# Turning attention probabilities outside TensorE: block transposes on VectorE and shifted copies on ScalarE

## The chip, the core and the metric

The kernel runs on one core of a Trainium2 chip. A core has TensorE (PE, the matrix engine; its weight loads are a row of their own, PEld), VectorE (DVE), ScalarE (ACT), GpSimd (POOL) and SyncE (SP, which here only issues DMAs). Each engine takes its instructions strictly in the order in which they were written for it, and waits where a semaphore tells it to. The metric is device time in microseconds. Three runs of the kernel before gave a median of 993.96 us (993.37 to 994.55).

## The reference

A decoder trunk of two layers on 256 tokens of width 2048, in float32: one Mamba-2 layer, then one sliding-window attention layer. Each is followed by a residual, DeepNorm scaling and a LayerNorm. The change lies wholly in the attention layer (and in the residual's affine part that runs beside it):

```python
def _swa_sink_attention(q, k, v, sinks):      # 256 tokens = 2 blocks of WINDOW = 128
    ...
    kk = jnp.concatenate([jnp.pad(kb, pad)[:, :-1], kb], axis=2)   # keys: block before, own block
    s = jnp.einsum("bcqhrd,bckhd->bchrqk", qb, kk).astype(jnp.float32) * (hd ** -0.5)
    ...
    valid = (diff >= 0)[None] & (diff < WINDOW)[None] & (kpos >= 0)
    s = jnp.where(valid[None, :, None, None], s, -jnp.inf)
    m = jnp.maximum(jnp.max(s, axis=-1, keepdims=True), sk)
    p = jnp.exp(s - m)
    p = p / (jnp.sum(p, axis=-1, keepdims=True) + jnp.exp(sk - m))
    o = jnp.einsum("bchrqk,bckhd->bcqhrd", p.astype(vv.dtype), vv)
...
    o = o * jax.nn.silu(gate)                 # in _swa_mixer
    return o @ w_out
```

There are 32 query heads of 64 in 4 groups (j = 0 to 3) of 8; each group shares one K/V head. In the first block a query sees only keys up to itself in that block. In the second block it sees 128 keys, some in the block before and the rest in its own. For every query exactly 128 key columns are live, and the second block packs the two parts into one 128-wide row.

## The kernel before, in words

**Products.** All large products are made in three passes of a split float32: a weight unit of 128 x 2048 is loaded (SP), ScalarE rounds it into a high part (`wh`, line 161), VectorE subtracts to get the low part (`wl`, line 164), and TensorE multiplies high by high, low by high and high by low (lines 249, 320 to 322, 973). There are four buffers each for `wh` and `wl`, and the weights are asked for two units ahead of the one in use. ScalarE and VectorE so have a standing duty for every unit, and TensorE takes the units one after the other.

**The attention layer** walks through `B_ORDER`: for each group j a `q` block (four units: the query projection), a `g` block (four units: the gate), and an `o` block (four units: the output projection), in the order q0 g0 q1 g1 o0 q2 g2 o1 q3 g3 o2 o3. After each unit, `tick()` counts down a list of delayed steps (`later(n, step)`), and so the attention steps of a group are put between two units of large products some ticks later. A tile scheduler then writes each engine's instructions in one fixed order.

**The attention steps of group j** (`attend(j, h)`, h = 0 and 1 for the two token blocks):

- Scores: 8 matmuls (h = 0, line 1090) or 16 (h = 1, line 1097) into PSUM tiles of the kind `ax`, of which there are four. This text calls them QK0 and QK1.
- h = 0: VectorE adds the mask on the way out of PSUM (line 1104). h = 1: ScalarE copies (line 1111), VectorE overwrites by predicate (line 1114).
- Softmax: VectorE takes the row maximum (1121) and three tiny steps (1122 to 1124), ScalarE makes eight exponentials with row sums (1127), VectorE adds, inverts and multiplies (1130 to 1132). This is `p`: queries on partitions, 8 heads x 128 keys along the row.
- Turn (`turn_p`, line 1136): the product with V needs keys on partitions. TensorE transposes eight 128 x 128 tiles against an identity (line 1140) into PSUM; VectorE and ScalarE take them out (1149, 1151 for h = 0; for h = 1 VectorE masks them twice, once for each of the two key blocks, line 1144) into tiles `pt`. This text calls the two turns of a group turn 0 and turn 1.
- PV (`pv`, line 1154): product with V (1161 for h = 0; 1178 and 1185 for h = 1), then VectorE multiplies by half the gate into `o` (1164, 1191), and ScalarE and VectorE split `o` into `oH` and `oL` for the output projection (1200, 1201).

**The residual** of the first LayerNorm's affine part (`residual`, lines 1022 and 1023) takes eight VectorE pairs between the units; its rows are fetched by POOL's DMA queue into a single pair of buffers `gb`.

## Time and profile before

| what | value |
|---|---|
| median of three runs | 993.96 us |
| the profiled execution | 993.77 us |
| its span, first to last instruction | 991.8 us |
| granted TensorE clock | 1.000 |
| busy: PE, PEld, DVE, ACT, POOL | 985.8, 897.4, 775.2, 566.5, 105.4 us |
| turns of probabilities on TensorE (line 1140) | 64 transposes in 8 turns, 8.4 us |

Times in a trace are counted from the start of the span. Rows of instruction groups name line, engine, operation, output and input tiles with buffer numbers left out, and shapes. A row of the timeline gives the start, the length and, in brackets, the idle time in front and what ended it. Matmuls overlap each other: a recorded length is longer than the distance to the next one, so TensorE's price of a step is read from distances between starts, or from the chain of waits, which counts each stretch of time once.

### The profile page before, as it was taken

What the parts mean: (1) busy time and instruction counts of PE and PEld (TensorE: products, weight loads), DVE (VectorE), ACT (ScalarE), POOL (GpSimd) and SP (SyncE); (2) the same over time, 40 slices, a digit from 0 to 9 for tenths busy, and PEclk for the clock granted to TensorE, in tenths of its full rate; (3) what the DMA queues carried; (4) which work ended last, traced back from release to release, by engine and by line L of the source; (5) the groups of instructions that cost most, each with busy time, mean ns of one, the idle gap of its engine ahead of it and who ended that gap; (6) DMA issues with size and microseconds to landing.
All of it is one profiled execution on the core that took longest, in us unless ns stands there. A gap on an engine that the chain in (4) does not pass through costs nothing.

```text
span 991.8 us, 18106 instructions
## 1 busy us (share of the span) xinstructions
PE 985.8 (99%) x7132; PEld 897.4 (90%) x7132; DVE 775.2 (78%) x1206; ACT 566.5 (57%) x992; POOL 105.4 (11%) x130
## 2 busy tenths in 40 slices
PE   9999999999999999999999999999999999999997
PEld 8999989999999998999999999888998978978976
DVE  7888897877786887686787687889688786686696
ACT  7585866547646654664664664566455544544542
POOL 0000303004003002100300300303100000000003
PEclk9999999999999999999999999999999999999999
DMA  9688577575576666656657466456754646456432
GB/s 363 241 270 328 164 262 223 172 236 176 193 232 187 219 207 196 208 180 209 208 170 236 139 203 215 157 178 223 253 185 154 192 159 197 158 159 196 158 128 86
DMA packets 61557, 198.90 MB, mean 201 GB/s; under 512 B 6848, under 2 KB 11360, under 8 KB 61216
## 3 DMA queue, kind: packets, MB, share of 16 engines
q1 hardware_dynamic: 58528, 188.53, 57.8%
q0 software_dynamic: 2336, 8.69, 2.7%
q8 instruction: 56, 0.92, 0.4%
q10 hardware_dynamic: 608, 0.52, 0.2%
q14 instruction: 29, 0.24, 0.1%
HBM read 195.49 MB, written 2.23 MB: 199 GB/s over the span
## 4 chain that ended last, share of the span: by engine, by line
PE 99%; DVE 0%; DVEq 0%; issue 0%
PE mm L249 53%; PE mm L973 11%; PE mm L320 9%; PE mm L321 9%; PE mm L322 9%; PE ax L628 2%; PE ax L604 1%; PE ax L1097 1%; PE ax L1090 0%; PE ax L587 0%; PE mm L387 0%; PE ax L1161 0%; PE ax L1140 0%; PE ax L1051 0%; PE ax L1178 0%; PE mm L1140 0%
## 5 line engine op out<-in xcount | busy, mean ns | idle before, releaser
L164 DVE TENSOR_TENSOR wl<-wr,wh 128x1024 fp32r<-128x1024 f32 (+2 forms) x338 | 393.1, 1182 | 103.6 <-ACT wh L161 101.5
L161 ACT ACTIVATE wh<-wr 128x1024 fp32r<-128x1024 f32 (+2 forms) x338 | 332.1, 1010 | 193.4 <-issue 69.1
L249 PE MATMUL mm<-xH,wh 128*128 128x256 f32 x1280 | 355.4, 278 | 0.0
L249 PE MATMUL mm<-xL,wh 128*128 128x256 f32 x1280 | 354.0, 277 | 0.0
L249 PE MATMUL mm<-xH,wl 128*128 128x256 f32 x1280 | 353.9, 277 | 0.0
L249 PEld LDWEIGHTS mm<-xH,wh 128*128 128x128 f32 x1280 | 240.4, 188 | 1.9 <-issue 0.5
L249 PEld LDWEIGHTS mm<-xL,wh 128*128 128x128 f32 x1280 | 240.6, 188 | 1.0
L249 PEld LDWEIGHTS mm<-xH,wl 128*128 128x128 f32 x1280 | 240.5, 188 | 0.2 <-DVE wl L164 0.2
L320 PE MATMUL mm<-wh,yH 128*128 128x512 f32 x256 | 101.4, 396 | 0.0
L321 PE MATMUL mm<-wh,yL 128*128 128x512 f32 x256 | 99.8, 390 | 0.0
L322 PE MATMUL mm<-wl,yH 128*128 128x512 f32 x256 | 99.7, 389 | 0.0
L644 POOL TENSOR_TENSOR yz<-yz,z 128x256 f32<-128x256 f32 x32 | 32.8, 1033 | 468.9 <-DVE yz L639 468.9
L249 PE MATMUL mm<-x1H,wh 128*128 128x256 f32 x256 | 71.7, 280 | 0.0
L491 DVE SCALAR_TENSOR_TENSOR cv<-mm,pc,cv 128x255 f32<-128x255 f32 x144 | 68.6, 477 | 3.3 <-ACT cv L489 1.9
L249 PE MATMUL mm<-x1L,wh 128*128 128x256 f32 x256 | 70.8, 277 | 0.0
L249 PE MATMUL mm<-x1H,wl 128*128 128x256 f32 x256 | 70.8, 276 | 0.0
L973 PE MATMUL mm<-wh,x1H 128*128 128x512 f32 x160 | 62.9, 393 | 0.0
L973 PE MATMUL mm<-wl,x1H 128*128 128x512 f32 x160 | 61.8, 389 | 0.0
L973 PE MATMUL mm<-wh,x1L 128*128 128x512 f32 x160 | 60.9, 389 | 0.0
L320 PEld LDWEIGHTS mm<-wh,yH 128*128 128x128 f32 x256 | 48.1, 188 | 10.3 <-DVE z L580 0.9
L322 PEld LDWEIGHTS mm<-wl,yH 128*128 128x128 f32 x256 | 48.0, 188 | 10.2
L321 PEld LDWEIGHTS mm<-wh,yL 128*128 128x128 f32 x256 | 48.1, 188 | 9.0
(226 smaller groups left out, 1346.8 us busy)
## 6 DMA issues: line engine op xcount, KB each, us to landing
wr<-in_wa SPq DMA_DIRECT2D x154, 512.0 KB, 5.0
wr<-in_wo SPq DMA_DIRECT2D x64, 512.0 KB, 4.4
wr<-in_wq SPq DMA_DIRECT2D x32, 512.0 KB, 4.5
wr<-in_wg SPq DMA_DIRECT2D x31, 512.0 KB, 4.7
wr<-in_wb SPq DMA_DIRECT2D x16, 512.0 KB, 4.1
wr<-in_wb SPq DMA_DIRECT2D x32, 256.0 KB, 3.7
rb<-rscr SPq DMA_DIRECT2D x11, 512.0 KB, 4.1
wr<-in_wkv SPq DMA_DIRECT2D x8, 512.0 KB, 4.9
```

The source lines that it names most:

```text
L161: m = nc.scalar.activation(h[:, sl], v, AF.Copy)
L164: m = nc.vector.tensor_tensor(l[:, sl], v, h[:, sl].bitcast(F32), ALU.subtract)
L249: m = nc.tensor.matmul(ps, a, b, start=first and i == 0, stop=last and i == 2)
L320: pinned(nc.tensor.matmul(ps, aH[:, k, hs], u.h[:, ks], start=k == 0 and add is None, stop=False), pin)
L321: pinned(nc.tensor.matmul(ps, aL[:, k, hs], u.h[:, ks], start=False, stop=False), pin)
L322: pinned(nc.tensor.matmul(ps, aH[:, k, hs], u.l[:, ks], start=False, stop=k == 3), pin)
L491: nc.vector.scalar_tensor_tensor(a[:, sft:], ps[:, : S - sft], w(3 - sft), a[:, sft:], ALU.mult, ALU.add)
L604: nc.tensor.transpose(ps[:, o : o + P], st.xs[i][:, c * P : (c + 1) * P], ident)
L628: nc.tensor.matmul(ps[64 * r : 64 * r + 64, cols], xd[:, c, r, :], e[:, 256:] if c else e[:, :256], start=c == 0, stop=c == 1,)
L644: nc.gpsimd.tensor_tensor(v, v, st.z[i][:], ALU.mult)
L973: m = nc.tensor.matmul(ps[:], (x1H, x1L, x1H)[i][:, kk, hs], (u.h, u.h, u.l)[i][:, ks], start=(kk, i) == (0, 0), stop=ui == 3 and (k, i) = ...
L1097: nc.tensor.matmul(pss[par][qs, at : at + 192], q2[rows, b + i, qs], kT[rows, j, 64 * part : 64 * part + 192], start=True, stop=True,)
```

## The change

In seven of the eight turns (all but j = 3, h = 1) TensorE makes no transposes. Instead:

- `p` is written in another arrangement: block column c (32 keys) outermost, then head, then key within the block. Softmax works on a strided view of it.
- VectorE turns every 32 x 32 block in place with one instruction per turn, from `p` to `z`, 128 x 1024 (`turn_far`, the STREAM_TRANSPOSE rows below). After that each block holds keys on partitions, but a block (query rows i, key columns c) still sits on the partitions of i.
- ScalarE copies each block to the partitions of c: one copy of 32 x 256 per pair (i, c); 16 for h = 1, and 10 for h = 0, where blocks above the diagonal are zero and are cleared once by three GpSimd memsets in a tile that is kept for this (`first_pt`).
- For h = 1 VectorE then makes the two masked parts from one SBUF tile (two instructions of 128 x 1024) where it made four of 128 x 512 from PSUM. For h = 0 the two copies out of PSUM (VectorE 1151, ScalarE 1149) are gone.
- The factor 0.5 of the gate moves into the reciprocal (one tiny VectorE instruction more per turn), and `o` is a plain product.
- Both PV products of a group now stand at the same tick (`PV_AT`), later than before for h = 0.
- The residual's steps are at other ticks (`RES_AT`), and its rows are fetched some ticks ahead of use (`GB_AT`, `load_affine`).
- Buffers: `p` and `z` share three, `o` takes the place of the query tiles `qt`, the bias rows have one buffer in place of two, and the last LayerNorm's temporary tiles use the tiles of the turn.

The last turn keeps TensorE's transposes, and writes its masked parts in the new arrangement. The diff, cut to its core:

```diff
-NPT = 6
 B_ORDER = [("q", 0), ("g", 0), ("q", 1), ("g", 1), ("o", 0), ("q", 2), ("g", 2), ("o", 1),
            ("q", 3), ("g", 3), ("o", 2), ("o", 3)]
 
-RES_AT = [1, 2, 3, 4, 9, 10, 11, 12]
+RES_AT = [2, 3, 6, 7, 11, 12, 14, 15]
+MOVE_AT, MASK_AT = [2, 2, 3, 3], 4
+PV_AT = [[8, 5], [5, 4]]
+GB_AT = [0, 4, 8, 13]
 ALPHA = (2.0 * 2) ** 0.25
...
+    def load_affine(c):
+        for i, n in enumerate(("lng", "lnb")):
+            gb1[i] = bp.tile([P, 512], F32, tag=f"gb{i}", name=nm("gb1"), bufs=1)
+            nc.gpsimd.dma_start(gb1[i][:], A[n][0, c * 512 : (c + 1) * 512].partition_broadcast(P))
     def residual(c, h):
 
-        if h == 0:
-            for i, n in enumerate(("lng", "lnb")):
-                gb1[i] = bp.tile([P, 512], F32, tag=f"gb{i}", name=nm("gb1"), bufs=1)
...
     gb1 = {}
+    load_affine(0)
     for c in range(4):
+        if c:
+            later(GB_AT[c], lambda c=c: load_affine(c))
         for h in range(2):
...
+    def first_pt():
+        if not firsts:
+            t = bp.tile([P, 4, 8, 32], F32, tag="pt0", name="pt0", bufs=1)
+            for c in range(1, 4):
+                nc.gpsimd.memset(t[32 * c : 32 * c + 32, :c].rearrange("p c r a -> p (c r a)"), 0.0)
+            firsts.append(t)
+        return firsts[0]
...
-        p = bp.tile([P, 8, P], F32, tag=f"p{h}", name=nm("p"), bufs=1)
+        p = bp.tile([P, 1024], F32, tag="p", name=nm("p"), bufs=3)
+        far = j < 3 or h == 0
+        byhead = p[:].rearrange("p (c r b) -> p r c b" if far else "p (r c b) -> p r c b", r=8, c=4)
...
-                v = p[:, par * 4 + b : par * 4 + b + per, :]
+                v = byhead[:, par * 4 + b : par * 4 + b + per]
+                got = pss[par][:].rearrange("p (a k) -> p a k", a=per)
                 if h == 0:
                     nc.vector.tensor_tensor(
...
+                        v, blocks(got), blocks(mask_a0.unsqueeze(1)).to_broadcast([P, per, 4, 32]), ALU.add
                     )
...
-        nc.vector.tensor_reduce(mx, p[:], AX.X, ALU.max)
+        nc.vector.tensor_reduce(mx, byhead, AX.XY, ALU.max)
...
             nc.scalar.activation(
-                p[:, r, :], p[:, r, :], AF.Exp, bias=ng[:, r : r + 1], accum_out=rs[:, r : r + 1]
+                byhead[:, r], byhead[:, r], AF.Exp, bias=ng[:, r : r + 1], accum_out=rs[:, r : r + 1]
             )
...
         nc.vector.reciprocal(ri, rs)
-        nc.vector.tensor_tensor(p[:], p[:], ri.unsqueeze(2).to_broadcast([P, 8, P]), ALU.mult)
+        nc.vector.tensor_scalar(ri, ri, 0.5, None, ALU.mult)
+        nc.vector.tensor_tensor(
+            byhead, byhead, ri.unsqueeze(2).unsqueeze(3).to_broadcast([P, 8, 4, 32]), ALU.mult
...
+        def turn_far():
+            z = bp.tile([P, 4, 256], F32, tag="p", name=nm("z"), bufs=3)
+            nc.vector.transpose(z[:].rearrange("p c f -> p (c f)"), p[:])
+            if h == 0:
+                pts[0] = first_pt()
+            else:
+                for kc in range(2):
+                    pts[kc] = bp.tile([P, 4, 8, 32], F32, tag=("pri", "own")[kc], name=nm("pt"), bufs=1)
+            def moved(c):
+                for i in range(c * (h == 0), 4):
+                    nc.scalar.copy(
+                        pts[0][32 * c : 32 * c + 32, i].rearrange("p r a -> p (r a)"), z[32 * i : 32 * i + 32, c]
+                    )
+            def parts():
+                t, own = (pts[kc][:].rearrange("p c r b -> p r c b") for kc in range(2))
+                for kc, d in ((1, own), (0, t)):
+                    nc.vector.tensor_tensor(d, t, masked(kc, 8), ALU.mult)
+            for c in range(4):
+                later(MOVE_AT[c], lambda c=c: moved(c))
+            if h:
+                later(MASK_AT, parts)
         def turn_p():
+            for kc in range(2):
+                pts[kc] = bp.tile([P, 4, 8, 32], F32, tag=("pri", "own")[kc], name=nm("pt"), bufs=1)
             for par in range(2):
-                pt = ax_tile() if h else mm_tile()
+                pt = ax_tile()
                 for a in range(4):
-                    nc.tensor.transpose(pt[:, a * P : (a + 1) * P], p[:, par * 4 + a, :], ident)
...
-                            (anti, tri)[kc].unsqueeze(1).to_broadcast([P, 4, P]), ALU.mult,
...
+                got = blocks(pt[:].rearrange("p (a q) -> p a q", a=4))
+                for kc in range(2):
+                    t = pts[kc][:].rearrange("p c r b -> p r c b")[:, par * 4 : par * 4 + 4]
+                    nc.vector.tensor_tensor(t, got, masked(kc, 4), ALU.mult)
...
+            def gated(ov, q0, n):
+                at = slice(h * P + q0, h * P + q0 + n)
+                nc.vector.tensor_tensor(
+                    blocks(o[:, :, q0 : q0 + n]), ov.rearrange("p (c a b) -> p a c b", a=4, b=32),
+                    blocks(sg[j][:, :, at]), ALU.mult,
+                )
...
                 for par in range(2):
...
                     )
...
+                gated(ov[:], 0, P)
...
-        last = j == 3
-        later(4 if last and h == 0 else 3, turn_p)
-        later((5 if last else 6) if h == 0 else (8 if 0 < j < 3 else 4), pv)
+        if far:
+            turn_far()
+        else:
+            later(3, turn_p)
+        later(PV_AT[j == 3][h], pv)
         if h == 0:
-            later(1 if last else 3, lambda: attend(j, 1))
+            later(1 if j == 3 else 3, lambda: attend(j, 1))
```

What the scheduler makes of it is seen at three places.

TensorE, group 0. Before, turn 1 stands right behind the first PV (line 1161), and the second PV stands a unit later, with the query transposes of group 1 (line 1051) behind it (`ax`: PSUM tiles, `pt`: turned probabilities, `cc`: the identity, `mm` ... `x1H`: large products):

```order
L973 MATMUL mm_8450<-wl_8558,x1H 128x512
L1161 MATMUL ax_8674<-pt_8498,vt 64x512
L1161 MATMUL ax_8674<-pt_8505,vt 64x512
L1140 MATMUL ax_8682<-cc,p_8507 128x128 x4
L1140 MATMUL ax_8691<-cc,p_8507 128x128 x4
L249 MATMUL mm_8731<-x1H,wh_8593 128x256
```

and a unit later the last rows of the second PV:

```order
L1185 MATMUL ax_8781<-pt_8698,vt 64x256
L1185 MATMUL ax_8782<-pt_8696,vt 64x256
L1051 MATMUL ax_8795<-cc,qt_8700 128x128 x4
L1051 MATMUL ax_8802<-cc,qt_8709 128x128 x4
L249 MATMUL mm_8823<-x1H,wh_8635 128x256
```

That unit lies between the two PV products, so the first one has been emptied long before the next scores need its tile.

Now both PV products (lines 1231, 1245, 1252) stand together, and the scores of group 1 (line 1114) directly behind them. They take five `ax` tiles in a row, of which there are four; the built program makes the second score tile (`ax_8878`) wait for VectorE, which has to empty the first PV tile (`ax_8855`):

```order
L1231 MATMUL ax_8855<-pt_8324,vt 64x512 x2
L1245 MATMUL ax_8862<-pt_8559,vt 64x256 x2
L1245 MATMUL ax_8863<-pt_8560,vt 64x256 x2
L1252 MATMUL ax_8862<-pt_8560,vt 64x256
L1252 MATMUL ax_8863<-pt_8559,vt 64x256
L1252 MATMUL ax_8862<-pt_8560,vt 64x256
L1252 MATMUL ax_8863<-pt_8559,vt 64x256
L1114 MATMUL ax_8877<-kT,qT_8778 128x128
L1114 MATMUL ax_8878<-kT,qT_8778 128x128
```

The two L1140 rows (eight transposes) are gone, and PV, PV and scores stand in one block with no large products between.

VectorE, the same place. Before, `o` of the first PV (line 1164) stands among the query rows of group 1:

```order
L963 TENSOR_TENSOR qt_8700<-rt_8702 128x8x8
L1045 TENSOR_TENSOR qt_8709<-mm_8450,bias_8451 128x512
L164 TENSOR_TENSOR wl_8812<-wr_8813,wh_8811 128x128
L958 TENSOR_TENSOR rt_8711<-qt_8709,cs 128x64
L1164 SCALAR_TENSOR_TENSOR o_8673<-ax_8674,sg_8156 128x512
L1144 TENSOR_TENSOR pt_8687<-ax_8682,cc 128x512
L1144 TENSOR_TENSOR pt_8689<-ax_8682,cc 128x512
L1201 TENSOR_TENSOR oL_8679<-o_8673,oH_8678 128x4x128
L1144 TENSOR_TENSOR pt_8696<-ax_8691,cc 128x512
```

The masked parts of turn 1 (line 1144) and everything of the next weight units stand behind it. Now `o` (line 1219) stands behind the two masked parts (line 1186), two whole weight units and the last residual steps (lines 1028, 1029):

```order
L1186 TENSOR_TENSOR pt_8559<-pt_8559,cc 128x8x4x32
L166 TENSOR_TENSOR wl_8790<-wr_8791,wh_8789 128x896
L166 TENSOR_TENSOR wl_8790<-wr_8793,wh_8789 128x1024
L1082 SCALAR_TENSOR_TENSOR sg_8705<-sg_8705,mm_8718 128x256
L1028 TENSOR_TENSOR xr<-xr,gb_1074_8767 128x512
L166 TENSOR_TENSOR wl_8912<-wr_8913,wh_8911 128x1024
L1029 TENSOR_TENSOR xr<-xr,gb_1075_8769 128x512
L166 TENSOR_TENSOR wl_8912<-wr_8915,wh_8911 128x1024
L1028 TENSOR_TENSOR xr<-xr,gb_1074_8767 128x512
L1029 TENSOR_TENSOR xr<-xr,gb_1075_8769 128x512
L1219 TENSOR_TENSOR o_8854<-ax_8855,sg_8150 128x512
```

So two residual pairs, nearly two weight units and the masked parts have moved from behind the emptying of the first PV tile to in front of it.

ScalarE and VectorE at the last group. Before, ScalarE goes from the score copies of h = 1 (line 1111) over three weight halves to the exponentials of h = 1 (line 1127):

```order
L1111 COPY p_10392<-ax_10409 128x256
L1111 COPY p_10392<-ax_10410 128x256
L161 ACTIVATE wh_10507<-wr_10509 128x1024
L161 ACTIVATE wh_10507<-wr_10512 128x1024
L161 ACTIVATE wh_10547<-wr_10549 128x1024
L1071 ACTIVATE sg_10144<-mm_10456 128x256
L1127 ACTIVATE p_10392,sm_10425<-p_10392,sm_10425 128x128 x4
```

There the exponentials stand behind three weight halves and a gate row. Now ten block copies (line 1179) and a weight unit (`wh_10575`) stand there ahead of the same exponentials (line 1151):

```order
L1134 COPY p_10409<-ax_10426 128x256
L1134 COPY p_10409<-ax_10427 128x256
L1179 COPY pt_8324<-z_10344 32x256 x7
L1081 ACTIVATE sg_10173<-mm_10474 128x256
L1179 COPY pt_8324<-z_10344 32x256 x3
L163 ACTIVATE wh_10575<-wr_10577 128x1024
L163 ACTIVATE wh_10575<-wr_10580 128x1024
L1369 ACTIVATE rr<-cc 128x128
L1151 ACTIVATE p_10409,sm_10442<-p_10409,sm_10442 128x128 x2
```

Ten block copies and one weight half more have moved in front of these exponentials. And VectorE has the block transpose ahead of the predicated copies, and the weight half `wl_10576`, which needs `wh_10575`, ahead of the row `sm` (line 1147) that those exponentials wait for:

```order
L1170 STREAM_TRANSPOSE z_10344<-p_10313 128x1024
L1137 COPY_PREDICATED p_10409<-cc,ax_10410 64x2x64 x2
L1137 COPY_PREDICATED p_10409<-cc,ax_10411 64x2x64 x2
L1137 COPY_PREDICATED p_10409<-cc,ax_10426 64x2x64 x2
L1137 COPY_PREDICATED p_10409<-cc,ax_10427 64x2x64 x2
L166 TENSOR_TENSOR wl_10533<-wr_10537,wh_10532 128x1024
L1145 TENSOR_REDUCE sm_10442<-p_10409 128x8
L1082 SCALAR_TENSOR_TENSOR sg_10173<-sg_10173,mm_10474 128x256
L1146 TENSOR_TENSOR sm_10442<-sm_10442,snk 128x8
L166 TENSOR_TENSOR wl_10576<-wr_10577,wh_10575 128x1024
L1147 TENSOR_SCALAR sm_10442<-sm_10442 128x8
L333 TENSOR_TENSOR xr<-xr,mm_10544 128x512
```

The transpose, and a weight half that waits for ScalarE's block copies, have moved in front of the exponentials of the last group.

## The prediction

> **What bounds the kernel now.** I read the page first, for the busy shares and the chain of waits:

> ```profile
> PE 985.8 (99%) x7132; PEld 897.4 (90%) x7132; DVE 775.2 (78%) x1206; ACT 566.5 (57%) x992; POOL 105.4 (11%) x130
> PE 99%; DVE 0%; DVEq 0%; issue 0%
> ```

> TensorE carries the whole chain. Since busy shares are means, I then read the attention stretch by stages (busy time of PE, PEld, DVE, ACT, POOL, then clock and DMA), here the stretch of turn 0 and QK1 of group 0 and that of the last group:

> ```profile
> 738.00:757.00 19.00, 19.00 (x114) 15.48 (x112) 15.50 (x31) 10.94 (x31) 1.08 (x2) 1.00 0.53 168
> 929.00:946.00 17.00, 17.00 (x106) 15.05 (x103) 13.95 (x27) 13.00 (x39) 1.06 (x2) 1.00 0.59 226
> ```

> TensorE has no gap in either. VectorE is 82% busy in both, so it is next in line. ScalarE is 58% busy in the first and 76% in the second, DMA about half. So TensorE work that goes away is worth its full price, unless TensorE then waits for VectorE or ScalarE. The chain of waits in time order gives that price, as it counts no overlap (start, length, what); group 0 first, then the last group:

> ```profile
> 738.38 0.88 PE mm L1140 x8
> 739.26 1.46 PE ax L1097 x32
> ...
> 757.28 1.01 PE ax L1161 x4
> 758.29 1.02 PE ax L1140 x8
> 759.31 5.47 PE mm L249 x48
> 764.78 1.01 PE ax L1178 x8
> 765.80 0.59 PE ax L1185 x8
> 766.39 1.02 PE ax L1051 x8
> 767.41 5.46 PE mm L249 x48
> ...
> 945.60 0.87 PE mm L1140 x8
> 946.47 0.87 PE ax L1140 x8
> ...
> 952.82 1.01 PE ax L1161 x4
> 953.83 0.86 PE ax L1178 x8
> ```

> **What is removed.** Turn 0 goes four times (0.88 three times, 0.87 in the last group), turn 1 three times (1.02): 2.64 + 0.87 + 3.06 = 6.57 us. The second PV costs 1.01 when it comes from large products (764.78) and 0.86 right behind the first one (953.83), as it now does in groups 0 to 2: 3 x 0.15 = 0.45. Together 7.0 us off TensorE.

> **What is added, and where it lies.** These groups of the attention stretch (busy us, mean ns) give the prices:

> ```profile
> L1132 DVE TENSOR_TENSOR p<-p,sm 128x1024 f32<-128x1024 f32 x8 | 9.8, 1219 | 0.1
> L1144 DVE TENSOR_TENSOR pt<-ax,cc 128x512 f32<-128x512 f32 x16 | 10.1, 680 | 0.0
> L1151 DVE COPY pt<-mm 128x512 f32<-128x512 f32 x4 | 2.7, 682 | 0.0
> L1114 DVE COPY_PREDICATED p<-cc,ax 64x128 f32<-64x128 uint32 x32 | 9.5, 298 | 0.4
> L1122 DVE TENSOR_TENSOR sm<-sm,snk 128x8 f32<-128x8 f32 x8 | 1.3, 160 | 0.0
> L1123 DVE TENSOR_SCALAR sm<-sm 128x8 f32<-128x8 f32 x8 | 1.4, 170 | 0.2
> L958 DVE TENSOR_TENSOR rt<-qt,cs 128x64 f32<-128x64 f32 x6 | 1.3, 221 | 0.1
> L1127 ACT ACTIVATE p<-p,sm 128x128 f32<-128x128 f32 x64 | 24.8, 389 | 34.8 <-DVE sm L1123 34.8
> 792.79 1.20 ACT L1111 COPY p<-ax 128x256 f32<-128x256 f32 x4
> 679.28 1.41 POOL L1003 COPY kd<-kd 128x256 f32<-128x256 f32 x1 [15.04 <-DVE kd L963]
> ```

> *Block transpose, seven of 128 x 1024.* No row shows one. The nearest is the 1024-element multiply, 1219 ns; the cheap end is the 0.68 us that 512 elements take. The dear end is the predicated copy: 298 ns for 128 elements, 8 x 298 = 2.4 us. I take 1.2, since a transpose has one input and one output of plain rows like the multiply.

> [...]

> *VectorE in all.* h = 0: -0.68 (L1151) + 1.22 + 0.17. h = 1: -4 x 0.68 + 1.22 + 0.17 + 2 x 1.22 for the masks, 1.1 us more in each of three. With 0.17 in the last turn, 4 x 0.71 + 3 x 1.1 + 0.2 = 6.3 us in some 240. The strided views cost nothing: rows of 8-element runs (L958, 64 elements, 221 ns) stand 61 ns above 8 elements (160), about 1 ns per element, as in dense rows.

> *ScalarE.* 4 x 10 + 3 x 16 = 88 block copies. Four copies of 256 columns take 1.20 us, so 0.30 each: 26 us, spread over ScalarE's idle third. The other bound is the exponential's 389 ns: 34 us.

> *GpSimd.* Three memsets, 1536 columns, stand ahead of a copy that waited 15 us for VectorE: at that copy's rate (256 columns in 1.41 us) they take 8.5, hidden. The earlier fetch of the residual's rows takes a VectorE wait away that TensorE never felt. Buffers and the 0.5 in the reciprocal: nothing.

> **First new wait: group 0.** QK0 of group 1 needs a fifth `ax` tile, so it waits until `o` has emptied the first PV. When TensorE gets there, in the old clock: the first PV begins at 757.28 - 0.88 = 756.4 plus what moved in between, two units (5.5 each) and the query turn (1.02), so 768.4; both PVs 1.01 + 0.86 + 0.59: 770.9. VectorE before:

> ```profile
> 751.10 0.17 DVE L1130 TENSOR_TENSOR sm<-sm 128x8 f32<-128x8 f32 x1 [3.22 <-ACT p L1127]
> 752.76 2.22 DVE L164 TENSOR_TENSOR wl<-wr,wh 128x896 fp32r<-128x896 f32 x2
> 754.89 0.69 DVE L1022 TENSOR_TENSOR xr<-xr,gb 128x512 f32<-128x512 f32 x1
> 755.50 0.28 DVE L164 TENSOR_TENSOR wl<-wr,wh 128x128 fp32r<-128x128 f32 x1
> 755.70 0.69 DVE L1023 TENSOR_TENSOR xr<-xr,gb 128x512 f32<-128x512 f32 x1
> 758.02 1.22 DVE L164 TENSOR_TENSOR wl<-wr,wh 128x1024 fp32r<-128x1024 f32 x1
> 759.16 0.22 DVE L958 TENSOR_TENSOR rt<-qt,cs 128x64 f32<-128x64 f32 x1
> 761.03 0.69 DVE L1164 SCALAR_TENSOR_TENSOR o<-ax,sg 128x512 f32<-128x512 f32 x1
> ```

> From 751.10 it runs without a pause. Start to start, a weight unit is 2.13 + 0.20 = 2.33, a 1024 half 1.14, a residual row 0.61. The new order puts between 751.10 and `o`: three weight units 7.0, two halves 2.3, six residual rows 3.7, the query rows of group 1 3.0 (two adds of 0.6, twelve of 0.14), multiply and transpose 2.3, two masks 2.3, tiny rows 0.5, a gate row 0.3: 21.4 us, to 772.5, and `o` ends at 773.1. Wait: 2.2 to 2.3 us. ScalarE is no later: its 16 copies run from 755.2, behind the transpose, to 760 (761.4 at 389 ns), and the masks come at 762.7. Groups 1 and 2 have large products behind PV, and the same walk from QK1 on (five units, 27 us) ends their masks some 6 us ahead of PV: no wait.

> **Second new wait: the last turn.** TensorE reaches it where turn 0 stood, 945.60. VectorE before:

> ```profile
> 930.53 0.17 DVE L1130 TENSOR_TENSOR sm<-sm 128x8 f32<-128x8 f32 x1 [3.15 <-ACT p L1127]
> 932.23 2.20 DVE L1114 COPY_PREDICATED p<-cc,ax 64x128 f32<-64x128 uint32 x7
> 942.29 1.22 DVE L1132 TENSOR_TENSOR p<-p,sm 128x1024 f32<-128x1024 f32 x1
> ```

> `p` was ready at 943.5, 3 us ahead of its turn at 946.47. In the new order, from 930.53: tiny rows and a gate row 1.0, multiply, weight half and transpose 3.45 (to 934.95), eight predicated copies 2.5, weight half and maximum 2.3, gate and tiny 0.4: 940.15. ScalarE makes its ten copies from 934.95 (3.0), a gate row 0.3 and the weight half 1.0 by 939.3, in time. Then the weight half 1.15 and a tiny row, 941.5; eight exponentials and sums 3.3 (VectorE waited 3.15 for those of h = 0, row above); three tiny rows and the multiply 1.8: 946.6. Wait: 1.0 us. Everything behind (PV, `o`, the last projection) has the same distances as before.

> **Sum.** The profiled execution took 993.77 us, 1.97 over its span and 0.19 under the median, so its sum stands for the median. 993.77 - 7.0 + 2.3 + 1.0 = 990.1 us.

> **Rivals.**
> - *No wait at all.* If VectorE reaches `o` 2.3 us sooner (transposes near 0.7, or shorter queues than I counted) and the last `p` 1.0 sooner, 993.77 - 7.0 = 986.8. For it: both margins are small sums of long queues. Against: each row in them has a price from this trace.
> - *Dear transposes.* At 2.4 us, two stand ahead of `o` in group 0 (the first delays ScalarE's copies and through them the splits) and one ahead of the last turn: 3 x 1.2 = 3.6 more, 993.7, no change.
> - *Slower: each 32 x 32 step pays an instruction's fixed price.* At 160 ns (the 8-element row) for 32 block columns, 5.1 us per transpose, 3.9 over mine: 990.1 + 3 x 3.9 = 1001.8. It decides from 2.4 us per transpose on, and from 3.0 the loss is over 0.2%. Against: it is one instruction, and no VectorE row quoted here costs more per element than the predicated copy (2.3 ns).
> - *The time comes back as waits for weights.* VectorE's 6.3 us and ScalarE's 26 delay the splits until TensorE waits for them; all 7 us return, 993.8. Against: the weights are asked for two units (11 us) ahead, and both waits above are shorter.

> **Chances.** Forecast with two short waits 0.52; no wait 0.20; dear transposes 0.13; slower 0.10; weights 0.05. A measurement of this kernel tells about 0.2% (2 us) from no change. Faster by more: 0.52 + 0.20 = 0.72; within: 0.13 + 0.05 = 0.18; slower: 0.10. The range 986.6 to 994.0 takes in all but the slower case and part of the weights'; the forecast's own is 988 to 992.

> **What would show it.** In the profile after: seven block transposes near 1.2 us (2.4 would make the third case); copies of 32 x 256 at 0.3 start to start; on TensorE 8 transposes left; a wait of about 2 us in front of line 1114 in group 1, released by VectorE's line 1219, and of about 1 us in front of line 1199, released by line 1157. Waits for `wh` or `wl` in front of large products would make me wrong, as would a PV that waits for its masks.

## The result, and the profile after

The changed kernel takes 992.77 us (median; 991.73 to 994.45), the kernel before, on the same chips, 993.84 us. The ratio is 0.999 (95% interval 0.9983 to 0.9996): 1.1 us faster, within the 0.2% that I called no change, and 2.7 us above the forecast of 990.1. The profiled execution took 992.29 us.

Busy times and the chain of waits of the changed kernel, from the page:

```profile
PE 979.4 (99%) x7076; PEld 892.2 (90%) x7076; DVE 781.1 (79%) x1211; ACT 599.4 (61%) x1076; POOL 103.5 (10%) x133
...
PE 92%; DVE 4%; ACT 2%; issue 1%; DVEq 0%; ACTq 0%
```

TensorE is 6.4 us less busy, VectorE 5.9 and ScalarE 32.9 more. Before, TensorE carried 99% of the chain; now VectorE and ScalarE have 6% of it. The list of what TensorE waited for in the attention stretch of the changed kernel (who waited, for whom: us in total, times, longest) says where:

```profile
PE ax L1061 <- DVE qt L965: 2.0, 1, 2.0
PE ax L1199 <- DVE p L1157: 1.7, 1, 1.7
PE ax L1114 <- DVE o L1219: 1.3, 1, 1.3
```

The second and third are the two waits of the forecast, the third shorter and the second longer than it had them. The first, the query turn of group 1, is one it did not have at all.

To put all runs on one scale I read distances on TensorE: from the start of the last large product ahead of an attention step to the start of the first one behind it, from K's transposes to the end of the last projection. A wait and a shorter step both show in it.

| place | before | after | after, without its wait |
|---|---|---|---|
| query turn of group 1 | (behind PV) | 3.14 | 0.91 |
| both PV and scores of group 1 | (other order) | 5.52 | 3.76 |
| last turn | 1.89 with turn 0 | 2.93 | 1.05 |
| all steps | 36.32 | 34.96 | 29.1 |

(0.91 is the query turn of groups 0, 2 and 3 after the change; 3.76 and 1.05 are from experiments below. The last row counts 19 steps before and 18 after.) So 7.2 us of TensorE are gone, as the forecast had it (7.0), and 2.2 + 1.8 + 1.9 = 5.9 us came back as waits.

The groups of the added instructions, in the attention stretch (busy us, mean ns, idle time in front and who ended it):

```profile
L1179 ACT COPY pt<-z 32x256 f32<-32x256 f32 x88 | 35.5, 404 | 7.0 <-DVE z L1170 5.9
L1157 DVE TENSOR_TENSOR p<-p,sm 128x1024 f32<-128x1024 f32 x8 | 9.8, 1225 | 0.3
L1145 DVE TENSOR_REDUCE sm<-p 128x8 f32<-128x1024 f32 x8 | 9.7, 1214 | 0.0
L1170 DVE STREAM_TRANSPOSE z<-p 128x1024 f32<-128x1024 f32 x7 | 8.7, 1238 | 0.0
L1186 DVE TENSOR_TENSOR pt<-pt,cc 128x1024 f32<-128x1024 f32 x6 | 7.3, 1222 | 4.3 <-ACT pt L1179 4.3
```

The block transpose costs what a 1024-element multiply costs (1238 ns; 1225 for the multiply), and the strided views are free, as taken (1225 ns for the multiply and 1214 for the maximum; 1219 and 1213 before). The block copies are dearer than taken: 0.40 us each for 0.30.

Now the place that was missed. First VectorE of the changed kernel in group 0, then ScalarE (start, length, what; in brackets the idle time in front and what ended it):

```profile
732.86 1.24 DVE L1170 STREAM_TRANSPOSE z<-p 128x1024 f32<-128x1024 f32 x1
734.02 2.32 DVE L166 TENSOR_TENSOR wl<-wr,wh 128x1024 fp32r<-128x1024 f32 x2
737.48 0.42 DVE L1082 SCALAR_TENSOR_TENSOR sg<-sg,mm 128x256 f32<-128x256 f32 x1 [1.14 <-ACT sg L1081]
739.82 3.56 DVE L166 TENSOR_TENSOR wl<-wr,wh 128x1024 fp32r<-128x1024 f32 x4 [1.91 <-ACT wh L163]
...
751.93 0.17 DVE L1154 TENSOR_TENSOR sm<-sm 128x8 f32<-128x8 f32 x1 [3.21 <-ACT p L1151]
...
763.40 0.22 DVE L965 TENSOR_TENSOR qt<-rt 128x64 f32<-128x64 f32 x1
...
773.28 0.68 DVE L1219 TENSOR_TENSOR o<-ax,sg 128x512 f32<-128x512 f32 x1
```

```profile
734.13 2.91 ACT L1179 COPY pt<-z 32x256 f32<-32x256 f32 x7 [0.78 <-DVE z L1170]
737.07 0.38 ACT L1081 ACTIVATE sg<-mm 128x256 f32<-128x256 f32 x1
737.48 1.23 ACT L1179 COPY pt<-z 32x256 f32<-32x256 f32 x3
738.73 3.05 ACT L163 ACTIVATE wh<-wr 128x1024 fp32r<-128x1024 f32 x4
...
756.07 6.65 ACT L1179 COPY pt<-z 32x256 f32<-32x256 f32 x16 [0.18 <-DVE z L1170]
```

TensorE starts its last large product ahead of the query turn at 761.0; the last rope row that it needs ends at 763.6. Upstream, ten block copies stand on ScalarE ahead of a gate row and a weight half, and VectorE waits 1.14 and 1.91 us for these. Sixteen copies take 6.65 us: 0.415 from start to start, with no overlap.

### The profile page after: what moved, and what is told of

Read it like the earlier page. It is cut to its first block, busy times and chain, and to the rows that moved or that the text cites. A ratio compares the mean times of both kernels' runs of the same rounds, so it can differ in the third digit from the quotient of the medians.

```text
span 990.3 us, 18070 instructions
## 1 busy us (share of the span) xinstructions
PE 979.4 (99%) x7076; PEld 892.2 (90%) x7076; DVE 781.1 (79%) x1211; ACT 599.4 (61%) x1076; POOL 103.5 (10%) x133
## 4 chain that ended last, share of the span: by engine, by line
PE 92%; DVE 4%; ACT 2%; issue 1%; DVEq 0%; ACTq 0%
PE mm L251 50%; PE mm L975 9%; PE mm L322 9%; PE mm L323 8%; PE mm L324 8%; PE ax L630 2%; DVE wl L166 1%; ACT p L1151 1%; PE ax L606 1%; ACT pt L1179 0%; PE mm L389 0%; PE ax L589 0%; ACT wh L163 0%; PE ax L906 0%; PE ax L1114 0%
## 5 line engine op out<-in xcount | busy, mean ns | idle before, releaser
L646 POOL TENSOR_TENSOR yz<-yz,z 128x256 f32<-128x256 f32 x32 | 32.5, 1024 | 468.6 <-DVE yz L641 468.6
L324 PEld LDWEIGHTS mm<-wl,yH 128*128 128x128 f32 x256 | 48.1, 188 | 10.1
L331 DVE SCALAR_TENSOR_TENSOR xr<-mm,r,xr 128x512 f32<-128x512 f32 x64 | 47.1, 745 | 11.7 <-PE mm L324 7.4
```

The source lines that it names most:

```text
L324: pinned(nc.tensor.matmul(ps, aH[:, k, hs], u.l[:, ks], start=False, stop=k == 3), pin)
L331: nc.vector.scalar_tensor_tensor(v, ps, rms[:, h : h + 1], v, ALU.mult, ALU.add)
L646: nc.gpsimd.tensor_tensor(v, v, st.z[i][:], ALU.mult)
```

## Experiments

All are made from the changed kernel (992.8 us, distances 34.96). The diffs are shortened; in them `issue_after(x)` puts what is in its block behind instruction x on that engine.

**Residual's last pair later.**

```diff
-RES_AT = [2, 3, 6, 7, 11, 12, 14, 15]
-GB_AT = [0, 4, 8, 13]
+RES_AT = [2, 3, 6, 7, 11, 12, 17, 18]
+GB_AT = [0, 4, 8, 16]
```

> Theory (three local waits): TensorE waits in three places because an instruction it needs stands late in VectorE's fixed order, and there is slack behind each. Here the residual's last pair of steps stands behind the first PV's emptying (`o`), so `o` comes 4 x 0.61 = 2.4 us sooner and the wait in front of the scores of group 1 (distance from the last large product to the next 5.52 us, 3.96 without a wait) goes: 1.5 us, 992.8 to 991.3. The query turn (3.14) and the last turn (2.93) stay as they are. Rival (backlog): VectorE is late as a whole, so what is taken from one wait comes back at the next place where TensorE needs VectorE: the distance shrinks here and another grows by as much, 992.8.

Measured: 993.99 us (ratio to before 1.0002, 0.9993 to 1.0011). What this TensorE waited for:

```profile
PE ax L1245 <- DVE pt L1186: 2.1, 1, 2.1
PE ax L1061 <- DVE qt L965: 2.0, 1, 2.0
PE ax L1199 <- DVE p L1157: 1.7, 1, 1.7
```

The wait at the scores went as expected (5.52 to 3.76), the other two stayed, and a new one came in group 1: the second PV waits for its masked parts (distance 2.78 to 5.09). The four residual steps (2.4 us) now stand in group 1's softmax, and its sixteen copies end later:

```profile
813.41 2.34 DVE L166 TENSOR_TENSOR wl<-wr,wh 128x1024 fp32r<-128x1024 f32 x2
819.62 1.23 DVE L1186 TENSOR_TENSOR pt<-pt,cc 128x1024 f32<-128x1024 f32 x1 [3.87 <-ACT pt L1179]
```

TensorE also comes 1.5 us sooner to group 1, with the wait at the scores gone. So the cause of the wait at the scores is VectorE's order, as in the theory, but the slack behind is small: the forecast's "some 6 us" in group 1 are about 1 us. By itself this run fits the rival as well, since 1.8 us went at one place and 2.3 came at the next; the runs below tell the two apart. In the changed kernel the second masked part there and the second PV stand like this:

```profile
819.34 1.22 DVE L1186 TENSOR_TENSOR pt<-pt,cc 128x1024 f32<-128x1024 f32 x1
```

```profile
821.52 1.03 PE L1245 MATMUL ax<-pt,vt 128*64 128x256 f32 x8
```

The part is done at 820.6, 1.0 us ahead.

**Query turn of group 1 a unit later.**

```diff
-            later(1, qtr)
+            pending.insert(h, [2, qtr]) if j in (1,) else later(1, qtr)
...
-            later(2, lambda j=j: attend(j, 0))
+            later(3 if j in (1,) else 2, lambda j=j: attend(j, 0))
```

> The query turn of group 1 stands a unit later, in front of both PV, and the scores of group 1 a unit later still; nothing is taken from any engine. Theory: TensorE comes to the query turn 5.5 us later, when VectorE's rope rows are done, and two units lie between the PV and the tiles that `o` must empty; both waits go (2.2 and 1.6 us), the last turn stays at 2.93: 992.8 - 3.8 = 989.0. Rival (backlog): VectorE is no sooner with its queue, and the PV waits for its masked parts or the later scores for `o`: 991.5 to 992.8.

Measured: 989.53 us (ratio 0.9959, 0.9947 to 0.9971). Two waits are gone, and a short one is new:

```profile
PE ax L1199 <- DVE p L1157: 1.7, 1, 1.7
...
PE ax L1245 <- ACT qT L1065: 0.6, 1, 0.6
```

Nothing was taken from any engine; 3.2 us came from the places of two steps alone, the query turn and the scores. The rest of the 3.8 is the 0.6 us that the fifth `ax` tile waits for ScalarE to empty the query turn.

**Last group: block copies behind the exponentials.**

```diff
+                with tc.issue_after(exps[0]) if j == 3 else ExitStack():   # last exponential of h = 1
                     for i in range(c * (h == 0), 4):
                         nc.scalar.copy(...)
...
-                later(MOVE_AT[c], lambda c=c: moved(c))
+                later(MOVE_AT[j == 3][c], lambda c=c: moved(c))    # MOVE_AT[1] = [4, 4, 4, 4]
```

> In the last group ScalarE's ten block copies stand behind the exponentials of h = 1 and no longer in front of them. Theory: the copies, 0.41 us each and not 0.30, cost the last turn only the 0.43 us that VectorE waited for a weight half behind them; the rest of the last wait is VectorE's own queue (the block transpose, 1.14 us, among it). The distance at the last turn goes from 2.93 to 2.5 us, the time from 992.8 to 992.4. Rival: ScalarE's copies are the whole of this wait: 2.93 to 1.04, 990.9.

Measured: 992.12 us (ratio 0.9984, 0.9975 to 0.9993); the distance went from 2.93 to 2.45. ScalarE's copies are 0.5 us of this wait, not the whole.

**Last group: the block transpose behind the row as well.** To the edit above comes:

```diff
-            nc.vector.transpose(z[:].rearrange("p c f -> p (c f)"), p[:])
+            # j == 3: two ticks later, behind line 1147 of h = 1
+            with tc.issue_after(srow[0]):
+                nc.vector.transpose(z[:].rearrange("p c f -> p (c f)"), p[:])
```

> As the run with the copies behind the exponentials, and VectorE's block transpose of the last group too stands behind the tiny row that the exponentials of h = 1 wait for. Theory: VectorE reaches that row 1.14 us sooner for the transpose and some more by the order that follows; `p` is ready about when TensorE comes: the distance at the last turn goes from 2.93 to 1.0 or 1.2 us, the time from 992.8 to 991.0. Rival (backlog): the transposed blocks are then late for PV of the last group (2.78 us now) or for weights behind it, and the time stays near 992.5.

Measured: 990.80 us (ratio 0.9971, 0.9960 to 0.9982), distance 1.06, PV behind it 2.92 for 2.78. The rest of the wait was VectorE's order.

**ScalarE's ten copies of h = 0 later, groups 0 to 2.**

```diff
+                with tc.issue_after(taken[0]) if h == 0 and j < 3 else ExitStack():   # last line 1134 of h = 1
                     for i in range(c * (h == 0), 4):
                         nc.scalar.copy(...)
...
-                later(MOVE_AT[c], lambda c=c: moved(c))
+                later(MOVE_AT[h == 0 and j < 3][c], lambda c=c: moved(c))    # MOVE_AT[1] = [4, 4, 4, 4]
```

> In groups 0 to 2 ScalarE's ten block copies of h = 0 stand behind its score copies of h = 1, in a stretch where it idles 5.8 us now, and no longer in front of a gate row and a weight unit. Only ScalarE's order changes. Theory: these copies (10 x 0.41 us) are what makes VectorE wait 1.14 us for a gate row and 1.91 us for a weight half in each group; without them VectorE is up to 3.05 us sooner with everything behind, the query rows of group 1 among it. The wait at the query turn goes (3.14 to 0.91), the one at the scores of group 1 stays in part, as TensorE comes 2.2 us sooner and `o` 3.05 (5.52 to about 4.8): 992.8 - 3.0 = 989.8. Rival: VectorE is held there by the weights' buffers or by the scores of h = 1, not by the copies; both distances stay, 992.8.

Measured: 989.98 us (ratio 0.9964, 0.9952 to 0.9977). The query turn's distance is 1.95, that of PV and scores 4.40: 2.3 us less, and VectorE's two pauses are 0.7 us in all. The row behind the exponentials of h = 1, at 751.93 in the changed kernel, starts at 749.88, though this execution is 0.3 us behind on TensorE there: 2.3 of the 3.05 us. At the query rows only about 1.2 us are left of that, since this order has a masked part (1.14 us) between them:

```profile
749.88 0.17 DVE L1155 TENSOR_TENSOR sm<-sm 128x8 f32<-128x8 f32 x1 [3.22 <-ACT p L1152]
...
761.22 1.22 DVE L1191 TENSOR_TENSOR pt<-pt,cc 128x1024 f32<-128x1024 f32 x1
762.36 0.22 DVE L964 TENSOR_TENSOR qt<-rt 128x64 f32<-128x64 f32 x1
762.49 0.22 DVE L965 TENSOR_TENSOR qt<-rt 128x64 f32<-128x64 f32 x1
```

So ScalarE's copies are the upstream cause of more than half of the two waits in group 0 (2.3 of 4.0 us). The profile puts what is left at the query turn down to ScalarE's `wh`; as the second row above ends 0.15 us ahead of the transposes, just as in the changed kernel, I read it as the same wait.

**Each block transpose twice.**

```diff
             nc.vector.transpose(z[:].rearrange("p c f -> p (c f)"), p[:])
+            nc.vector.transpose(z[:].rearrange("p c f -> p (c f)"), p[:])
```

> Each block transpose is made twice into the same tile, which adds 1.14 us (start to start) of VectorE per turn and nothing else. Theory: three waits with little slack elsewhere; two transposes stand ahead of the query rows and of `o` in group 0 (2.3 us), one ahead of the last turn (1.1), and group 1 and 2, whose masked parts now end 0.8 and 1.3 us ahead of the second PV, pay 2 x 1.14 less that (1.5 and 1.0): 5.9 us in all, 998.7. Rival (as the forecast had it, groups 1 and 2 with 6 us of slack): 3 x 1.14 = 3.4, 996.2.

Measured: 1000.89 us (ratio 1.0076, 1.0063 to 1.0088). The distances grew by 5.1 us: query turn 3.94, scores 5.74, PV of groups 1 and 2 4.19 and 3.82, last turn 4.55. That is near the 5.9 in all, and groups 1 and 2 pay 2.5, as the small slack says. Group 0 pays only 1.0 of the 2.3 expected, in part because the scheduler put one residual row (0.6 us) behind `o` there, and the last turn 1.6 for 1.1. The other 3 us are the clock (below).

**All turns on TensorE, in the new order.** `far = False`; `turn_p` also takes h = 0, out of PSUM by VectorE and ScalarE.

> All eight turns on TensorE again, with everything else as in the changed kernel: its ticks, buffers, residual, the order of both PV, the strided arrangement of `p`; h = 0 taken out of PSUM by VectorE and ScalarE as before the change. Theory: the new order alone costs nothing; TensorE makes its 7.0 us again, comes later to each place and waits nowhere for more than 0.5 us: 993.8, as before. Rival: the new order itself brings waits (the fifth tile in front of the scores of group 1, 1.5 us or more, independent of the block transposes): 995.3 or more.

Measured: 996.62 us (ratio 1.003, 1.0018 to 1.0041). This put turn 0 in `ax` tiles; the scores of h = 1 behind it waited for one of them, three times:

```profile
PE ax L1121 <- ACT pt L1211: 1.3, 3, 0.5
```

So a run with `mm` tiles, as before the change:

```diff
-                pt = ax_tile()
+                pt = ax_tile() if h else mm_tile()
```

> The run with all turns on TensorE once more, with turn 0 in the PSUM tiles `mm`, as before the change, and not in `ax`. There the three turn 0 with the scores of h = 1 behind them took 3.67, 3.58 and 3.58 us where they take 2.66 before the change, as those scores waited for ScalarE to empty an `ax` tile. Theory: with that gone (2.85 us) the distances add up to 36.3 us as before the change, and the time is 993.8: the new order by itself costs and gains nothing. Rival: the new order brings the wait by itself; 996 or more.

Measured: 994.16 us, against 993.21 for the kernel before beside it (ratio 1.001, 1.0001 to 1.0019). Distances 36.98, 0.7 above before: 1.3 more in the last group, where a large product waits for VectorE to empty its tile, and a little less elsewhere. The query turn has 0.91, PV and scores 3.77: with TensorE's turns back in front, nothing waits there. The new order alone costs 0.1 to 1.9 us by the interval; the waits of the changed kernel come from VectorE's and ScalarE's added work and from TensorE's earlier arrival.

**Block copies as activations.**

```diff
-                    nc.scalar.copy(d, z_)
+                    nc.scalar.activation(d, z_, AF.Copy)
```

> ScalarE's 88 block copies are written as activations (function Copy) and not as copies; everything else is the changed kernel. One reading of 0.41 us a copy, start to start, is that a copy of this form does not overlap with the next, while activations from SBUF do (two of 128 x 1024 take 2.00 us at 1.05 each): then they take 0.30 here, 26 us in all, and the waits of the query turn, of the scores and of the last turn shrink by up to 1.0, 0 and 0.4 us: 992.8 to 991.5. The other reading: a source in SBUF, or 32 partitions, sets it, and nothing changes: 0.41, 992.8.

Measured: 993.01 us (ratio 0.9997, 0.9988 to 1.0006). The form changes nothing for the better:

```profile
L1179 ACT ACTIVATE pt<-z 32x256 f32<-32x256 f32 x88 | 36.6, 416 | 6.9 <-DVE z L1170 5.9
```

Whether the source in SBUF or the 32 partitions set the price, no run here tells apart.

**Both together.** The query turn a unit later, and the last group's transpose and copies later.

> The query turn of group 1 a unit later (as in the run that did only this) together with the last group's block transpose and copies behind the row and the exponentials of h = 1 (as in that run). All seven block transposes stay. Theory: the waits are independent, so the gains add: 989.5 - 1.9 = 987.6, with one wait of 0.6 us left in front of the second PV of group 0. Rival (backlog): what is taken in group 0 comes back in the last group, 989.5.

Measured: 987.83 us (ratio 0.9945, 0.9932 to 0.9959), distances 29.96. All that is left of TensorE's waits in the attention stretch:

```profile
PE ax L1259 <- ACT qT L1067: 0.3, 1, 0.3
```

The gains add, so the waits of group 0 and that of the last group are separate, and the rival (a backlog that moves on) is refuted for these places. This version beats both kernels, by 6.0 and 4.9 us.

**The clock.** The run with activations had a unit of large products of 7.0 us behind the query turn, in place of 5.4, at a granted clock of 0.50 for 3.4 us (which hid its wait at the scores: 3.93 for 5.52, and no time won). So two kernels were profiled once more as they were.

> The changed kernel as it is, profiled once more, to see whether the clock falls behind its waits. In the run with the block copies as activations the granted clock fell to 0.50 for 3.3 us (765.3 to 768.6) behind a wait of 2.3 us at the query turn, which made a unit of large products 1.6 us longer; in the first profile of the changed kernel it stayed at 1.00 behind a wait of 2.2 us. If that depends on where a wait falls and not on its length, some executions show it and some don't: then this one shows either 992.3 again, or one or two units 1.6 us longer and 993.9 to 995.5. The three waits themselves are the same in either case (distances 3.14, 5.52 and 2.93 us).

> The run with the residual's last pair later, profiled once more. Its distances added up to 0.6 us more than the changed kernel's, its median was 1.2 us above. If a fallen clock behind one of its waits (2.2, 2.3 and 1.9 us) is in part of its executions, this one shows a unit 1.6 us longer in one place or none; the distances stay at 3.14, 3.76, 5.09 and 2.93 us.

Measured: the changed kernel 992.34 us, no fall, distances 34.92. The one with the residual later 994.32 us, distances 35.48 as before (35.52), but its span 992.5 for 991.1. The same four microseconds behind the query turn, in its first and its second profile (behind the counts: granted clock, DMA share, GB/s):

```profile
764.00:768.00 4.00, 3.93 (x35) 3.96 (x36) 4.00 (x5) 4.00 (x7) 0.00 (x0) 1.00 0.84 280
```

```profile
764.00:768.00 4.00, 4.00 (x23) 4.00 (x22) 4.00 (x5) 4.00 (x6) 0.00 (x0) 0.57 0.82 273
```

The same kernel after the same wait ran once at full clock and once at half for 3.4 us, and the unit took 1.6 us longer. The run with doubled transposes shows it twice, behind waits of 2.0 us at the scores and 3.5 us at the last turn, and not behind one of 3.0 us at the query turn:

```profile
777.00:781.00 4.00, 4.00 (x23) 4.00 (x22) 4.00 (x7) 0.63 (x1) 0.00 (x0) 0.57 0.28 110
954.00:959.00 5.00, 5.00 (x19) 4.18 (x20) 4.58 (x7) 0.40 (x1) 0.00 (x0) 0.66 0.40 140
```

The falls fit a grid of 3.413 us. The recorded stretch at full clock up to the first change is 983.04 us in the first profile of the changed kernel and 986.45 in that of the kernel before, 288 and 289 such steps. From the end of a fall to the next change there are 221.9 us, 65 steps, both in the second profile with the residual later (768.0 to 989.8) and in the run with activations (768.7 to 990.6). Two steps around the wait at the query turn, first from the second profile with the residual later, then from the first profile of the changed kernel (behind the length: busy TensorE; third from the end: granted clock):

```profile
761.15:764.56 3.41, 1.39 (x13) 1.19 (x13) 3.41 (x9) 3.34 (x7) 0.42 (x1) 1.00 0.76 189
764.56:767.98 3.42, 3.42 (x19) 3.42 (x18) 3.42 (x5) 3.42 (x6) 0.00 (x0) 0.50 0.80 283
```

```profile
759.34:762.76 3.42, 2.39 (x22) 2.15 (x20) 3.42 (x12) 3.29 (x10) 1.07 (x2) 1.00 0.85 283
762.76:766.17 3.41, 2.40 (x21) 2.43 (x22) 3.41 (x7) 3.41 (x5) 0.00 (x0) 1.00 0.87 219
```

In the first the whole wait lies in one step, which idles for 2.0 us, and the next step runs at 0.50. In the second a border cuts the same wait into 1.0 and 1.0 us, and the clock stays. The wait of 3.0 us with doubled transposes was cut too, into 1.2 and 1.4. So the place of a wait against these steps fits all the runs. Idle time alone gives no threshold, though: the four steps ahead of the falls idle for 1.5 (the one with PV and scores in it), 2.0, 2.1 and 2.7 us, and one of 1.8 us (the last turn of the run with activations) kept the clock.

## Why the forecast was right and wrong, step by step

- **What is removed, 7.0 us:** right. The distances without waits are 7.2 us shorter, and c. 6 us of it can be had (the run with both edits).
- **Block transpose 1.2 us:** right: 1.238 for one instruction over 1024 columns of float32, beside 1.219 for the multiply whose row it was taken from. The rival "dear transposes" did not come, and its price was too small: doubled, they cost 5.1 us in waits, and 8.1 with the clock, and not 3.6.
- **"Four copies of 256 columns take 1.20 us, so 0.30 each":** the mis-sized term. They take 0.415 from start to start, 36 us in all. The row is four copies of 128 x 256 from PSUM that overlap (0.27 us apart at 0.39 long); these, of 32 x 256 from SBUF, are 0.404 long and don't. The other bound (0.389, an exponential from SBUF) was the nearer row.
- **"ScalarE is no later":** the step that failed first. I followed its sixteen copies of h = 1, not the ten of h = 0, which stand ahead of work that VectorE waits for. The walk of VectorE began at 751.10, behind that point, and took its start as given; in the changed kernel the same row starts at 751.93, though TensorE is 0.6 us ahead of its old times there, from the first step on. That is 1.4 us late. Moving those ten copies alone (in groups 0 to 2) made this row 2.3 us sooner and gave 2.8 us, 2.3 of it in the distances.
- **First new wait, 2.2 to 2.3 us at the scores:** place and releaser right, but 1.8 us came there on top of 2.2 at the query turn of the same group, 4.0 in all. The walk passed the query rows of group 1, and I asked only when `o` is reached. TensorE needs those rows ahead of that: without turn 1 and the first PV in front it is at the query turn at 761.2, where it came at 766.4. This omission alone would not have changed the sum, since what TensorE waits at the query turn it is later at the scores. By the forecast's own numbers the rows come at about 762.8 (11.7 us behind the start of the walk, as in the trace) and are needed at about 762.4 (756.4 and 5.5, and half of the turn), an estimate: some 0.5 of the 2.3 us would have stood at the query turn. The walk's length was right, 22.0 us from its start to the end of `o`, forecast and measured. Of the 1.7 us that were missing, 1.4 are its late start behind ScalarE's copies.
- **Groups 1 and 2, "some 6 us ahead":** wrong and for the time harmless: 1.0 us in group 1, as moving 2.4 us of residual into it showed at once (2.3 us of wait). In the trace VectorE pauses there behind ScalarE's copies: 0.5 and 1.9 us for a gate row and a weight half, and 2.1 us for the sixteen copies ahead of the masks.
- **Second new wait, 1.0 us at the last turn:** place and releaser right, 1.9 us. The copies are 0.5 of the missing 0.9; the other 0.4 are small pieces of the walk (TensorE a little sooner, exponentials and tiny rows a little longer) that no run tells apart.
- **GpSimd, VectorE in all, the weights, the strided views:** right. The three memsets took 1.6 us for the 8.5, hidden as forecast, and VectorE 5.9 us more for the 6.3; TensorE waits for neither `wh` nor `wl` in front of a large product in the profile after.
- **The sum:** 993.8 - 7.2 + 2.2 + 1.8 + 1.9 = 992.5, against 992.8 measured. The range held it, but the forecast's own band, 988 to 992, did not, and 0.72 of the chance stood on a gain of more than 0.2%. The upper end of the range stood for dear transposes and waits for weights, and neither came; that it held the result is in part luck.

## What to carry to other kernels

When work leaves an engine that bounds, compute its new arrival at every later step that needs another engine, in order, and compare each with when that is ready; the first such step is the first candidate for a wait, not the one with the scarce buffer. Begin the walk of the other engine ahead of the first instruction that was added, on it or on an engine that it waits for: here a walk of the right length began 1.4 us late. A long run of small instructions on a "free" engine delays what stands behind it in its fixed order, and through it the engine next in line (ten copies on ScalarE held VectorE back 2.3 us here): put it where that engine idles. When a change gives less than it removes, look for steps that can stand a unit later before taking work out.
